# S5 parameter preparation inside a two-layer decoder trunk: dense products on VectorE, block copies on ScalarE, an earlier begin and a quota of elements

## The chip, the core and the metric

One core of a Trainium2 chip runs the whole kernel. The metric is device time in microseconds (us) of one execution, the median over runs. The kernel computes in float32; a weight or activation is split into two float32r parts (high and low), and a product of two such numbers is made of three matmuls.

## What is computed

The reference is a trunk of two layers on 256 tokens of width 1024. Each layer is a feed-forward (half weight), a mixer, and another feed-forward:

```
x = x + 1/2 W_down( silu(g) * u ),  [g u] = RMSNorm(x) W_gu        # 2816 features
x = x + W_out [ S5(u), latent attention ]                          # mixer of layer 0
x = x + 1/2 feed-forward;  x = x + 1/2 feed-forward
x = x + differential attention;  x = x + 1/2 feed-forward;  RMSNorm
```

S5 is a diagonal state-space model of 32 groups with 64 complex states and 16 channels each. With dt = exp(log_dt), a = exp(lambda dt) and f = (a - 1) / lambda its input matrix is f B, its states follow x[t] = a x[t-1] + f B u[t], and its output is Re(C x[t]) + D u[t]. All of a, f and the matrices below depend on parameters alone, not on the tokens. The kernel works on blocks of four steps, so it needs, for each of 16 pairs of groups:

- E: a^(3-i) f B for i = 0..3, which carries four inputs into the state at the end of a block (e_re, e_im, transposed);
- W: C a^d for d = 1..4, which carries a block's first state to its four outputs (w_re, w_im);
- T: Re(C a^(i-i') f B) within a block, with D on the diagonal (tmat);
- cos and sin of n theta and |a|^4, for the scan over 64 blocks (cosn, sinn, mag4).

Making these is "the preparation". They are first read in the mixer of layer 0.

## The kernel before

A planner class `Weights` (L30) streams the weights: `load` (L45) issues a DMA of 512 KB on SP into one of five stage buffers; `pre` (L54) splits a piece of 1024 columns, the high half by a ScalarE copy (L69), the low half by a VectorE subtraction (L71), and asks for the next piece. In a few places GpSimd makes the low half of a second piece.

A feed-forward (`ffn`, L264) begins with `begin` (L220): the norm of token tile 0 (`residual`, `normed`), the last products of the phase before, the transposes of tile 0 into feature-major halves yh and yl (`transpose_split`, `halves`), then the same for tile 1; `finish` transposes tile 1. The first two feature tiles are done one token tile at a time (`early`, `gate`, `turn`, L294 to L323). Then come 20 feature tiles, f = 2 to 21 (L327): 48 "up" products into gu, silu on ScalarE (L340), a product on VectorE (sh), the split of it (hs), and, two feature tiles later, 12 "down" products into acc (L280). So TensorE reads what ScalarE and VectorE make of a feature tile only two tiles later; in `early`, `gate` and `turn` there is no such distance.

The preparation is a Python generator, `setup` (L1261): the rotary tables (`rope_tables`, L445), `mixer_constants` (L424), `s5_prep` (L495). It is the `background` of the first feed-forward. After each feature tile, `ffn` advances it by a number of yields: 4 each for f below 8, 2 each below 16, 5 each below 21, and all that are left (99) at f = 21 (L351 to L354). `tc.issue_after(last)` puts what the block issues on VectorE behind `last` (the low half of hs); the other engines' instructions are not held by it. The framework then orders each engine's queue by its own estimates of readiness and by the order of the program; on the chip every queue runs strictly in order.

`s5_prep` first makes a, its powers 1 to 4 and the tables by doubling, out of operations of 16 columns and then larger ones. exp is a power of e on GpSimd (`exp_start`, L388). Then f B is made in blocks: a pair's two groups lie in the two halves of the partitions and in columns 0 to 15 and 16 to 31, with zeros elsewhere, so operations work on 64 partitions (L601) or on blocks that are half zero. The E matrices are made for eight pairs at a time with 256-column operations (L651 to L656) in the room of w_re for the first eight pairs and of w_im for the last eight; `turned_inputs` (L613) transposes them on TensorE, ScalarE copies them into e_re and e_im, and products with C give the diagonals t0 for T. Afterwards GpSimd fills w_re and w_im with the W matrices, three 512-column operations for each of eight parts (`outputs_of`, L635 to L642). Last, ScalarE places the ten blocks of tmat (L677). Helpers record their operations under their own lines: tt is L118, stt L121, ts L124.

Of the kernel before, what the change touches and what calls it, by code (L numbers as in the profile page):

```python
# [29 lines left out]
class Weights:  # L30
    """A stream of weight chunks: loaded ahead, each split exactly into two float32r parts."""
# [7 lines left out]
    def plan(self, specs):  # L39
        """specs: (array [128, n], whether it goes to the wide buffers) in the order of use"""  # L40
# [13 lines left out]
    def pre(self, other=None):  # L54
        """Splits the next chunk; other: an engine that helps with its second half."""
# [32 lines left out]
def trunk(ctx: ExitStack, tc: tile.TileContext, x, pos, invf, wff, gains, w_u, w_cq, w_ckv,  # L88
          w_uq, w_ukv, w_glu, w_out0, w_in1, w_out1, s5_lam, s5_bc, s5_d, s5_bglu, qn, kvn,
          lamv, subln, out):  # L90
    nc = tc.nc
# [24 lines left out]

    def tt(out, a, b, op):
        return nc.vector.tensor_tensor(out=out, in0=a, in1=b, op=op)  # L118

    def stt(out, a, s, b, op0, op1):  # L120
        return nc.vector.scalar_tensor_tensor(out=out, in0=a, scalar=s, in1=b, op0=op0, op1=op1)  # L121

    def ts(out, a, s1, s2_, op0, op1):
        return nc.vector.tensor_scalar(out=out, in0=a, scalar1=s1, scalar2=s2_, op0=op0, op1=op1)  # L124
# [6 lines left out]
    def behind_both(last):  # L131
        """Work that is issued after two instructions on their engines."""
# [35 lines left out]
    def rsqrt(out, a):  # L168
        """out = a ** -0.5, one column or more."""
# [14 lines left out]
    def transpose_split(src, nk, hi, lo, t):  # L184
        """token-major src [128, nk*128] -> feature-major halves, columns of token tile t."""
# [9 lines left out]
    # Phases hand the residual stream over one token tile at a time: a phase's last products for tile 0  # L195
    # come first, and those for tile 1 run while tile 0 is normalised for the next phase.
# [23 lines left out]
    def begin(prev, row):  # L220
        """prev: (last products of tile 0, those of tile 1 in pieces, the accumulators, a factor, next chunks,
# [21 lines left out]
        if acc is None:  # L243
            with tc.issue_after(last):
                ups.append(W.pre(nc.gpsimd))
# [1121 lines left out]
```

## Time and profile before

Three runs took 1045.62 to 1045.81 us, median 1045.69. The profile is of one execution; the page gives its span, 1044.7 us, and no time of its own, so about 1.0 us lie around the span.

| | share of the span |
|---|---|
| TensorE (PE) busy | 1012.1 us, 97% |
| VectorE (DVE) busy | 635.2 us, 61% |
| ScalarE (ACT) busy | 494.1 us, 47% |
| GpSimd (POOL) busy | 101.4 us, 10% |
| chain that ended last | PE 85%, DVE 6%, issue 3%, ACT 3%, POOL 1%, DMA 1% |

A busy share is a mean over stages. The first feed-forward runs from the start to about 220 us; the mixer of layer 0 follows. Where TensorE is busy without a gap at the full clock, the work of the other engines costs nothing; where it has a gap or a lower clock, the entry "idle before <- releaser" of the timeline names whom it waited for. In a timeline each entry is a run of like instructions; matmuls overlap, so the distance between two starts is the price, not the duration.

### The profile page before, as it was taken

How to read it: one execution, taken by the hardware profiler on the slowest of the kernel's cores; microseconds unless marked ns; L12 is line 12 of the kernel's file. 1: busy time of each engine (PE TensorE's matmuls, PEld its weight loads, DVE VectorE, ACT ScalarE, POOL GpSimd, SP SyncE). 2: the span in 40 equal slices, each digit the busy share in tenths (PEclk: the TensorE clock that was granted, in tenths of full speed). 3: DMA queues.
4: the chain of work that ended last, by engine and by line, in shares of the span. 5: the costliest groups of instructions: out<-in, count | busy, mean ns of one | idle time of the engine just before them, and what ended most of it. 6: DMA issues, size and time to landing. Idle time of an engine off the chain costs nothing.

```text
span 1044.7 us, 16739 instructions
## 1 busy us (share of the span) xinstructions
PE 1012.1 (97%) x6730; PEld 928.3 (89%) x6730; DVE 635.2 (61%) x1117; ACT 494.1 (47%) x848; POOL 101.4 (10%) x115
## 2 busy tenths in 40 slices
PE   7999998999979999999999999999999999999997
PEld 6999997989878899999989999999888879999996
DVE  5788778365877865555447455543757776555432
ACT  5454542455636664444336444442567756444431
POOL 3210006601510100000010000000101110000000
PEclk9999997899969999999999999999999999999999
DMA  8866663135113585555627565563453448556521
GB/s 270 262 186 196 189 190 101 51 117 187 61 41 111 192 302 182 182 184 186 209 68 263 168 217 185 189 190 140 143 180 122 143 133 290 184 184 192 187 80 40
DMA packets 49807, 174.93 MB, mean 167 GB/s; under 512 B 6081, under 2 KB 7105, under 8 KB 49730
## 3 DMA queue, kind: packets, MB, share of 16 engines
q1 hardware_dynamic: 48720, 170.46, 50.8%
q10 hardware_dynamic: 1010, 3.41, 0.9%
q8 instruction: 52, 0.85, 0.3%
q14 instruction: 25, 0.20, 0.1%
HBM read 172.80 MB, written 1.05 MB: 166 GB/s over the span
## 4 chain that ended last, share of the span: by engine, by line
PE 85%; DVE 6%; issue 3%; ACT 3%; POOL 1%; DMA 1%; SPq 0%; POOLq 0%; DVEq 0%; ACTq 0%
PE gu L336 43%; PE acc L280 22%; PE proj L685 6%; PE gt L300 3%; DVE wlo L71 2%; PE acc L696 2%; PE pu L685 1%; DVE tmat L118 1%; PE pt L190 1%; DMA xr<-in_x_dram 1%; PE ckv L685 1%; PE pz L976 1%; PE cq L685 1%; PE yp L944 1%; ACT y L199 1%
## 5 line engine op out<-in xcount | busy, mean ns | idle before, releaser
L71 DVE TENSOR_TENSOR wlo<-stage,whi 128x1024 fp32r<-128x1024 f32 x230 | 287.8, 1259 | 244.1 <-ACT whi L69 243.9
L69 ACT CAST whi<-stage 128x1024 fp32r<-128x1024 f32 (+1 forms) x236 | 240.4, 1030 | 292.5 <-issue 237.6
L336 PE MATMUL gu<-yh,whi 128*128 128x256 f32 x1280 | 363.1, 284 | 0.0
L336 PE MATMUL gu<-yh,wlo 128*128 128x256 f32 x1280 | 363.0, 284 | 0.0
L336 PE MATMUL gu<-yl,whi 128*128 128x256 f32 x1280 | 362.8, 283 | 0.0
L336 PEld LDWEIGHTS gu<-yh,whi 128*128 128x128 f32 x1280 | 246.2, 192 | 2.7
L336 PEld LDWEIGHTS gu<-yl,whi 128*128 128x128 f32 x1280 | 246.2, 192 | 2.7
L336 PEld LDWEIGHTS gu<-yh,wlo 128*128 128x128 f32 x1280 | 246.1, 192 | 0.0
L280 PE MATMUL acc<-dhi,hs 128*128 128x512 f32 x704 | 193.7, 394 | 0.0
L280 PEld LDWEIGHTS acc<-dhi,hs 128*128 128x128 f32 x704 | 128.1, 190 | 23.3 <-ACT hs L127 0.3
L71 DVE TENSOR_TENSOR dlo<-stage,dhi 128x1024 fp32r<-128x1024 f32 x88 | 108.3, 1232 | 36.3 <-ACT dhi L69 35.8
L69 ACT CAST dhi<-stage 128x1024 fp32r<-128x1024 f32 x88 | 92.3, 1050 | 68.8 <-DMA stage<-in_wff_dram 68.6
L280 PE MATMUL acc<-dlo,hs 128*128 128x512 f32 x352 | 110.9, 391 | 0.0
L280 PEld LDWEIGHTS acc<-dlo,hs 128*128 128x128 f32 x352 | 66.4, 189 | 14.4
L170 POOL TENSOR_TENSOR rs<-rs,mhalf 128x1 f32<-128x1 f32 x14 | 7.8, 557 | 658.4 <-DVE rs L124 658.4
L118 DVE TENSOR_TENSOR sh<-sh,gu 128x256 f32<-128x256 f32 x80 | 33.1, 414 | 31.8 <-ACT sh L340 31.8
L118 DVE TENSOR_TENSOR hs<-sh,hs 128x256 fp32r<-128x256 f32 x80 | 35.6, 445 | 18.7 <-ACT hs L127 18.6
L340 ACT ACTIVATE sh<-gu 128x256 f32<-128x256 f32 x80 | 30.3, 379 | 31.3 <-PE gu L336 31.3
L127 ACT CAST hs<-sh 128x256 fp32r<-128x256 f32 x80 | 32.3, 403 | 16.9 <-DVE sh L118 16.9
L685 PE MATMUL proj<-whi,yh 128*128 128x512 f32 x96 | 38.7, 403 | 0.2 <-ACT yh L127 0.2
L685 PE MATMUL proj<-wlo,yh 128*128 128x512 f32 x96 | 37.5, 391 | 0.0
L300 PE MATMUL gt<-whi,yh 128*128 128x256 f32 x128 | 34.7, 300 | 2.7 <-ACT yh L127 2.6
(326 smaller groups left out, 1138.7 us busy)
## 6 DMA issues: line engine op xcount, KB each, us to landing
stage<-in_wff_dram SPq DMA_DIRECT2D x264, 512.0 KB, 4.6
stage<-in_w_in_dram SPq DMA_DIRECT2D x24, 512.0 KB, 4.4
stage<-in_w_out_dram SPq DMA_DIRECT2D x16, 512.0 KB, 3.7
gain<-in_gains_dram ACTq DMA_DIRECT2D x6, 512.0 KB, 4.9
stage<-in_w_u_dram SPq DMA_DIRECT2D x4, 512.0 KB, 4.7
xr<-in_x_dram SPq DMA_DIRECT2D x2, 512.0 KB, 5.2
stage<-in_w_cq_dram SPq DMA_DIRECT2D x2, 512.0 KB, 4.1
stage<-in_w_ckv_dram SPq DMA_DIRECT2D x2, 512.0 KB, 4.7
```

Source lines behind the costliest of these rows:

```text
L69: nc.scalar.copy(out=hi[:, c:c + w], in_=t[:, :w])
L71: eng.tensor_tensor(out=lo[:, c:c + w], in0=t[:, :w], in1=hi[:, c:c + w].bitcast(F32), op=ALU.subtract)
L118: return nc.vector.tensor_tensor(out=out, in0=a, in1=b, op=op)
L127: copy = nc.scalar.copy(out=hi, in_=src)
L190: nc.tensor.transpose(pt[:, k, :], src[:, (k0 + k) * 128:(k0 + k + 1) * 128], ident)
L199: return nc.scalar.activation(out=y[:, sl], in_=xr[t][:, sl], func=AF.Square, scale=1.0 / 32.0, accum_out=ms[:, c:c + 1]).ins
L280: nc.tensor.matmul(acc[t][c], a[:, sl], w[:, c * 512:(c + 1) * 512], start=(f == 0 and n == 0), stop=(f == NF - 1 and n == 2))
L300: last = nc.tensor.matmul(o, a[:, k, sl], w[:, k * 256:(k + 1) * 256], start=(k0 == 0 and n == 0), stop=(k0 > 0 and n == 11))
L336: nc.tensor.matmul(gu[:, s * 256:(s + 1) * 256], w[:, k, s, :], a[:, k, :], start=(k == 0 and n == 0), stop=(k == KT - 1 and n == 2))
L340: nc.scalar.activation(out=sh[:, 0, :], in_=gu[:, :256], func=AF.Silu)
L685: last = nc.tensor.matmul(acc, a[:, k0 + k, sl], w[:, k * width:(k + 1) * width], start=(k0 == 0 and n == 0), stop=(k0 + per == nk and n = ...
L696: mm = nc.tensor.matmul(acc[t][c], a[:, k0 + k, sl], w[:, o:o + 512], start=(first and k == 0 and n == 0), stop=(last and k == 1 and n == 2))
```

## The change

- VectorE alone makes the products of the preparation, dense: all 16 pairs and all 128 partitions at once, without the zeros (`cmul_halves` on 256 columns for f B, `powers` on 768 columns for the three E powers and 1024 for the four W powers).
- `apart` on ScalarE copies the dense result into the two blocks, two copies of 64 partitions each, with the sign where one is needed. GpSimd keeps the memsets and the powers of e.
- w_re and w_im hold all E matrices, then all W matrices. `turned_inputs` works on four pairs at a time.
- The generator is given out by `aside` (until a sum of elements per partition plus 140 per tt, stt or ts reaches a quota): 3000 behind the first norm of tile 0 in the first `begin`, 2500 behind the transposes of tile 1 in `finish`, 2400 after each feature tile, and the rest at f = 21. `pause` makes a feature tile give out one step and no more.
- lam, pos and the inverse frequencies are loaded on ScalarE's DMA queue before anything else. mag4 and the second columns of cosn and sinn are copied by ScalarE.

```
+    spent = [0]
+
+    def spend(out):
+        spent[0] += math.prod(out.shape[1:]) + 140
+
     def tt(out, a, b, op):
+        spend(out)
         return nc.vector.tensor_tensor(out=out, in0=a, in1=b, op=op)
...
+    def aside(background, quota, last):
+        if background is None:
+            return
+        with tc.issue_after(last):
+            spent[0] = 0
+            while spent[0] < quota:
+                if next(background, background) is background:
+                    break
...
         if acc is None:
             with tc.issue_after(last):
                 ups.append(W.pre(nc.gpsimd))
+        aside(background, 3000, last)
         for f in second:
             f()
...
                 for _ in range(more - 1):
                     ups.append(W.pre())
+            aside(background, 2500, last[1])
             return last
...
-            if background is not None:
-                with tc.issue_after(last):
-                    for _ in range(4 if f < 8 else 2 if f < 16 else 5 if f < NF - 1 else 99):
-                        next(background, None)
+            aside(background, 2400 if f < NF - 1 else 1 << 30, last)
...
+    def first_loads():
+        nc.scalar.dma_start(out=lam, in_=s5_lam)
+        nc.scalar.dma_start(out=posi, in_=pos)
+        nc.scalar.dma_start(out=inv, in_=invf.partition_broadcast(128))
...
+        for z in (w_re, w_im):
+            nc.gpsimd.memset(z, 0.0)
...
+        for i in range(3):
+            nc.scalar.copy(out=down[:, :, i, :], in_=pw[:, :, 2 - i, :])
...
-        nc.vector.tensor_copy(out=mag4, in_=m4.unsqueeze(2).to_broadcast([128, NPAIR, NBLK]))
-        nc.vector.memset(mag4[:, :, 0:1], 0.0)
+        nc.scalar.copy(out=mag4, in_=m4.unsqueeze(2).to_broadcast([128, NPAIR, NBLK]))
+        nc.gpsimd.memset(mag4[:, :, 0:1], 0.0)
...
+        yield from cmul_halves(b_re, b_im, bc[:, 0], bc[:, 1], frb, fib, u1, u2)
+
+        def apart(dst, src, scale=1.0):
+            for j in range(2):
+                r = slice(64 * j, 64 * j + 64)
+                nc.scalar.activation(out=dst[r, :, :, 16 * j:16 * j + 16], in_=src[r], func=AF.Copy, scale=scale)
...
+        def powers(out, x, y, sx, sy, table, m, u, op):
+            sh = [128, NPAIR, m, 16]
+            for o, v, s_ in ((out, x, sx), (u, y, sy)):
+                tt(o, v.unsqueeze(2).to_broadcast(sh),
+                   table[:, s_, :m].rearrange("p d q -> p q d").unsqueeze(3).to_broadcast(sh), MUL)
+                yield
+            tt(out, out, u, op)
...
+        for dst, own, x, y, sx, sy, op in ((p_re, b_re, b_re, b_im, 0, 1, SUB), (p_im, b_im, b_re, b_im, 1, 0, ADD)):
+            yield from powers(e3, x, y, sx, sy, down, 3, u3, op)
+            apart(dst[:, :, :3], e3)
+            apart(dst[:, :, 3:], own.unsqueeze(2))
             yield
...
+        def turned_inputs(q0):
+            for src, dst in ((w_re, e_re), (w_im, e_im)):
+                tp = bank("pt").rearrange("p (k c) -> p k c", c=128)
+                for k in range(4):
+                    nc.tensor.transpose(tp[:, k, :], src[:, q0 + k], ident)
+                nc.scalar.copy(out=dst[:, q0:q0 + 4, :], in_=tp)
...
+        def pause():
+            spent[0] += 1 << 20
             yield
+        yield from pause()
+        for q0 in range(0, NPAIR, 4):
+            turned_inputs(q0)
+            yield from pause()
...
-            nc.gpsimd.tensor_tensor(out=w, in0=c_re, in1=a, op=MUL)
-            nc.gpsimd.tensor_tensor(out=g, in0=c_im, in1=b, op=MUL)
-            nc.gpsimd.tensor_tensor(out=w, in0=w, in1=g, op=ADD)
...
+        for dst, sx, sy, op, scale in ((p_re, 0, 1, SUB, 1.0), (p_im, 1, 0, ADD, -1.0)):
+            yield from powers(wd, bc[:, 2], bc[:, 3], sx, sy, pw, 4, u4, op)
+            apart(dst, wd, scale)
             yield
...
+    first_loads()
     state = (lambda: None, [], None, 1.0, [], 1)
     state = ffn(state, gains[0], setup())
```

## Rows read from the trace of the kernel before

**Rows 1.** page, slices of 26.1 us: granted TensorE clock in tenths.
```profile
PEclk9999997899969999999999999999999999999999
```

**Rows 2.** windows: us, busy (count) of PE, PEld, DVE, ACT, POOL; clock, DMA share, GB/s.
```profile
9.20:26.00 16.80, 14.93 (x106) 14.62 (x105) 12.10 (x14) 11.00 (x17) 5.25 (x3) 1.00 0.82 264
26.00:156.00 130.00, 130.00 (x926) 122.61 (x924) 105.35 (x292) 61.60 (x91) 12.81 (x12) 1.00 0.67 204
156.00:205.00 49.00, 44.10 (x272) 41.31 (x272) 30.36 (x30) 12.60 (x20) 34.91 (x25) 0.79 0.29 86
```

**Rows 3.** the same windows view, 5 us within the first dip.
```profile
175.00:180.00 5.00, 2.76 (x13) 2.07 (x11) 2.97 (x4) 0.59 (x1) 1.93 (x2) 0.50 0.42 133
```

**Rows 4.** timeline of TensorE: start us, us, instruction, [idle before <- releaser].
```profile
153.97 1.03 PE L618 MATMUL pt<-ident,w_re 128*128 128x128 f32 x8
...
159.16 0.36 PE L336 MATMUL gu<-yh,whi 128*128 128x256 f32 x1
...
167.29 0.61 PE L280 MATMUL acc<-dlo,hs 128*128 128x512 f32 x2
170.57 1.08 PE L618 MATMUL pt<-ident,w_im 128*128 128x128 f32 x4 [2.66 <-DVE w_im L118]
...
178.15 1.08 PE L618 MATMUL pt<-ident,w_im 128*128 128x128 f32 x4 [2.24 <-DVE w_im L118]
...
194.96 0.28 PE L336 MATMUL gu<-yh,whi 128*128 128x256 f32 x1
```

**Rows 5.** chain that ended last in order of time, 140 to 235 us: start, us, what.
```profile
142.88 2.75 PE acc L280 x12
...
195.12 5.75 PE gu L336 x48
```

**Rows 6.** timeline of VectorE, two operations of 256 columns.
```profile
141.82 0.43 DVE L118 TENSOR_TENSOR w_re<-tmat 128x256 f32<-128x256 f32 x1
...
163.25 1.16 DVE L118 TENSOR_TENSOR w_im<-tmat 128x256 f32<-128x256 f32 x1
```

**Rows 7.** timeline of GpSimd, the first of its products.
```profile
159.47 4.66 POOL L640 TENSOR_TENSOR w_re<-cb,s5sc 128x512 f32<-128x512 f32 x4 [80.77 <-PE t L624]
```

**Rows 8.** groups by shape, VectorE, 78 to 156 us: busy, mean ns, idle before.
```profile
L71 DVE TENSOR_TENSOR wlo<-stage,whi 128x1024 fp32r<-128x1024 f32 x20 | 24.4, 1222 | 11.8 <-ACT whi L69 11.8
```

**Rows 9.** groups by shape, ScalarE, 0 to 220 us.
```profile
L69 ACT CAST whi<-stage 128x1024 fp32r<-128x1024 f32 x46 | 47.7, 1046 | 53.2 <-issue 42.8 <-PE gu L336 7.7 <-DMA stage<-in_wff_dram 1.5
```

**Rows 10.** chain that ended last in order of time, 0 to 45 us.
```profile
2.66 6.81 DMA xr<-in_x_dram
...
11.35 5.31 PE gt L300 x24
...
26.42 5.76 PE gu L336 x48
```

**Rows 11.** windows around the two small loads of before.
```profile
12.00:14.00 2.00, 2.00 (x11) 2.00 (x11) 1.77 (x4) 1.68 (x2) 0.46 (x2) 1.00 0.56 123
14.00:16.00 2.00, 2.00 (x11) 2.00 (x10) 2.00 (x2) 0.00 (x0) 2.00 (x1) 1.00 1.01 406
```

**Rows 12.** timeline of VectorE: two independent operations, then two dependent ones.
```profile
50.69 0.17 DVE L461 COPY cc<-co 128x8 f32<-128x8 f32 x1
50.76 0.17 DVE L462 COPY cc<-co 128x8 f32<-128x8 f32 x1
...
51.65 0.17 DVE L121 SCALAR_TENSOR_TENSOR s5r<-s5kh,s5r 128x16 f32<-128x16 f32 x1
51.85 0.17 DVE L121 SCALAR_TENSOR_TENSOR s5r<-s5k,s5r 128x16 f32<-128x16 f32 x1
```

**Rows 13.** powers on GpSimd (timeline); what VectorE waited for, 26 to 60 us.
```profile
37.25 2.95 POOL L389 TENSOR_TENSOR s5w<-euler,lam 128x16 f32<-128x16 f32 x1 [21.12 <-DMA lam<-in_s_lam_dram]
40.69 4.00 POOL L389 TENSOR_TENSOR s5w<-euler,s5t 128x16 f32<-128x16 f32 x1 [0.50 <-DVE s5sc L118]
...
DVE s5sc L118 <- POOL s5w L389: 1.5, 1, 1.5
```

More of the change, by code (lines that the diff above doesn't have):

```diff
@@ L264, in ffn @@
     def ffn(prev, row, background=None):
-        yh, yl, ups, finish = begin(prev, row)
+        yh, yl, ups, finish = begin(prev, row, background)
         acc = [[None, None], [None, None]]
@@ L443, in mixer_constants @@
         ts(nlam, nlam, LAM_INIT, 1.0, SUB, MUL)
+    posi = cst.tile([128, 2], I32, name="posi")
+    inv = cst.tile([128, 24], F32, name="inv")
+    lam = cst.tile([128, 3, NPAIR], F32, name="lam")
+    def first_loads():
+        nc.scalar.dma_start(out=lam, in_=s5_lam)
+        nc.scalar.dma_start(out=posi, in_=pos)
+        nc.scalar.dma_start(out=inv, in_=invf.partition_broadcast(128))
     def rope_tables():
-        posi = cst.tile([128, 2], I32, name="posi")
-        nc.sync.dma_start(out=posi, in_=pos)
-        inv = cst.tile([128, 24], F32, name="inv")
-        nc.sync.dma_start(out=inv, in_=invf.partition_broadcast(128))
         posf = small("posf", 2)
@@ L495, in s5_prep @@
     def s5_prep():
-        lam = cst.tile([128, 3, NPAIR], F32, name="lam")
-        nc.sync.dma_start(out=lam, in_=s5_lam)
         bc = s4("bc", [128, 4, NPAIR, 16])
@@ L533, in s5_prep @@
         yield
[L535 to L536 removed]
+        ar, ai = ({d: pw[:, s, d - 1, :] for d in range(1, 5)} for s in range(2))
         t1, t2 = tmp("t1", n), tmp("t2", n)
@@ L555, in s5_prep @@
         cmul(er, ei, dr, di, dr, di, t1, t2)
-        nc.vector.memset(cosn[:, :, 0:1], 1.0)
-        nc.vector.memset(sinn[:, :, 0:1], 0.0)
-        nc.vector.tensor_copy(out=cosn[:, :, 1:2], in_=er.unsqueeze(2))
-        nc.vector.tensor_copy(out=sinn[:, :, 1:2], in_=ei.unsqueeze(2))
+        nc.gpsimd.memset(cosn[:, :, 0:1], 1.0)
+        nc.gpsimd.memset(sinn[:, :, 0:1], 0.0)
+        nc.scalar.copy(out=cosn[:, :, 1:2], in_=er.unsqueeze(2))
+        nc.scalar.copy(out=sinn[:, :, 1:2], in_=ei.unsqueeze(2))
         yield
@@ L644, in s5_prep @@
-        behind = iter(())
-        for q0 in range(0, NPAIR, 8):
-            q = slice(q0, q0 + 8)
-            held = (w_re, w_im)[q0 // 8].rearrange("p q c -> p (q c)")
-            p_re, p_im = (held[:, o:o + 1024].rearrange("p (q i c) -> p q i c", q=8, i=4) for o in (0, 1024))
-            nc.scalar.copy(out=p_re[:, :, 3, :], in_=b_re[:, q])
-            nc.scalar.copy(out=p_im[:, :, 3, :], in_=b_im[:, q])
-            for i in range(3):
-                for _ in cmul_halves(p_re[:, :, i, :], p_im[:, :, i, :], b_re[:, q], b_im[:, q],
-                                     ar[3 - i][:, q].unsqueeze(2).to_broadcast(sh),
-                                     ai[3 - i][:, q].unsqueeze(2).to_broadcast(sh), u1, u2):
-                    next(behind, None)
-                    yield
-            for _ in behind:
-                yield
-            behind = turned_inputs(q0, p_re, p_im)
@@ L660, in s5_prep @@
-        for d in range(1, 5):
-            next(behind)
-            outputs_of(w_re, d)
-            yield
-        for d in range(1, 5):
-            outputs_of(w_im, d)
+        def turned_inputs(q0):
[4 more added lines that the diff above has]
+                nc.scalar.copy(out=dst[:, q0:q0 + 4, :], in_=tp)
+            for k in range(q0, q0 + 4):
+                nc.tensor.matmul(t0[:, k, :], w_re[:, k], c_re[:, k, :], start=True, stop=False)
+                nc.tensor.matmul(t0[:, k, :], w_im[:, k], nci[:, k, :], start=False, stop=True)
```

69 lines of the change are left out of this document (21 added, 48 removed).

## The prediction

> **What bounds the kernel now.** I read the slices of the page first, then the windows, then TensorE's timeline where they differ, then the chain, and last the engines that the wait names. The clock line of the page has two dips [rows 1]; the change touches only the first, which lies at the end of the first feed-forward (20 feature tiles, f = 2 to 21, with the S5 preparation as its background). From 26 to 156 us TensorE is busy all the time at the full clock, although VectorE, ScalarE and GpSimd work on the preparation meanwhile; from 156 to 205 us it lacks 4.9 us of work and has a mean granted clock of 0.79 [rows 2]. So the preparation costs nothing until its last fifth, and then it costs twice: TensorE stands still, and afterwards it is granted half the clock (1.2 instead of 2.4 GHz) for about 20 us; one stretch of that is shown [rows 3].
>
> The timeline says what the stop is. TensorE waits 2.66 us and 2.24 us in front of its transposes for w_im, which VectorE makes [rows 4] (until the W matrices are filled, w_re and w_im each hold half of the E matrices). The price, from the same rows: between the end of one group of down products (167.29 + 0.61 = 167.90) and the feature tile that begins at 194.96 pass 27.06 us. TensorE does three things in them: the second half of the preparation's transposes and products, whose first half took 159.16 - 153.97 = 5.19 us at the full clock; one set of 12 down products, 2.75 us; one set of 48 up products, 5.75 us [rows 4, 5]. At the full clock that is 13.69 us. **The loss is 27.06 - 13.69 = 13.4 us**: 4.9 us of waits and 8.5 us of half clock.
>
> Why VectorE was late: an operation of 256 columns took 0.43 us at 142 us, and 1.16 us at 163 us [rows 6]. In the second case GpSimd was running its 512-column operations of `outputs_of`, one of which holds that engine for over a microsecond [rows 7]. The last feature tile gives out all that is left ("99"), GpSimd has nothing queued ahead of it and starts at 159.5 us, four feature tiles before that code's place. VectorE has to serve the split of the weights in the same queue, so they slip as well.
>
> **The change, part by part.** The predicted time is the median of 1045.69 less what goes, plus what comes. The profiled execution has a span of 1044.7; about 1.0 us lie around it, which I carry over.
>
> *The tail.* No elementwise product of the preparation is left on GpSimd, only memsets and powers, so the 1.16 us operations should be 0.43 again. I counted the quota through the generator (elements per partition plus 140 for each tt, stt and ts). The first `aside` gives out 41 VectorE instructions, the second 20; f = 2 to 9 carry 2580 to 3312 units each, f = 10 and 11 the three E powers each (2724), f = 12 the first pause, f = 13 to 16 one block of transposes each, f = 17 and 18 the W powers (3492 each), f = 19 the last 1304 and ten copies. Nothing is left for f = 20 and 21: there is no dump at the end. TensorE still does the same 32 transposes and 64 small products (2 x 5.19 us), but their inputs were written a feature tile earlier, so no wait stands in front of them. VectorE per feature tile: three weight splits at 1.22 and two operations of 256 columns at 0.43 are 4.5 us; the largest background, three operations of 1024 columns, is 3.7 us more [rows 6, 8]. 8.2 us fit under the 8.5 us (5.75 + 2.75) that TensorE needs per tile, narrowly. ScalarE gets `apart`, eight copies of at most 1024 columns for the W matrices at no more than 1.05 us each [rows 9], two tiles apart; the down products wait two tiles, which hides a late one. If that cover went, one stop as in rows 4 would be back (rival 3). This part: **-13.4 us**.
>
> *The loads.* lam, posi and inv leave SP, where they were issued among the weight pieces, for ScalarE's queue, ahead of the gain row. Three issues before the gain delay the broadcast of the gain, and with it the second half of y0; the first feature tile does not start with that, though: the chain of the first 45 us runs from the second half of x, landed at 9.47, over its squares to the first products at 11.35 [rows 10]. So only what delays that transfer counts. By bytes, 37 KB at 406 GB/s are 0.1 us. By the row in which small loads run, 12 to 14 us, the engines are 0.56 busy at 123 GB/s where 406 GB/s take 1.01 [rows 11]: 0.25 too much over 2 us, 0.5 us for two of the three, 0.7 us for all. I take the upper end, 0.7, since the x transfer is in flight in the same microseconds. Here the Trainium skill (DMA: Bandwidth & Descriptors, section Queues, rings and completion order) says that each DMA engine takes packets in turn from the rings of SP and ScalarE, so a load on ScalarE's ring does not line up behind SP's; by that the term is the 0.7, and by strict order of issue it would be the 0.1. The other constants are now issued behind the first five weight pieces on SP, a megabyte that SP used to issue later; what is queued behind them are pieces that wait for a free stage buffer anyway. Nothing is charged for them.
>
> *The early start.* This part costs. 61 small VectorE instructions move into the stretch from 9.2 to 26 us, where TensorE has no two tiles of slack: yl, y1, the low half of the second weight chunk and the first gate are each needed within about a microsecond. VectorE is idle there for 16.80 - 12.10 = 4.7 us [rows 2]. Independent small operations follow each other at 0.07 us, dependent ones at 0.20 us [rows 12]; some 32 of the 61 are in the two sine chains and other dependent lines. All at 0.07 are 4.3 us, under the idle time: 0. All at 0.20 with nothing between are 12.2, that is 7.5 us over it. As counted, 32 x 0.20 + 29 x 0.07 = 8.4, 3.7 over; of that I take half, 1.8 us, because the main line's operations can be issued between the links of a chain. So **+0.7 + 1.8 = +2.5 us**, with ends at 0.1 and 8.2.
>
> *The rest.* mag4, cosn, sinn and the C copies go to ScalarE or GpSimd. ScalarE is busy for 61.6 of 130 us in that stretch [rows 2], and the copies are read tiles later: nothing. The doubled `down` copy of the powers likewise.
>
> Forecast: 1045.69 - 13.4 + 2.5 = **1034.8 us**.
>
> **The rivals.**
> 1. *The start is free* (0.1): 1045.69 - 13.4 + 0.1 = 1032.4. For it: VectorE's 4.7 idle microseconds. Against: they are spread over 17 us, and a dependent line of small operations does not wait for a gap.
> 2. *VectorE waits for GpSimd's powers at the start*: 2.95 and 4.00 us on GpSimd for 16 columns; even in the slack stretch VectorE stood 1.5 us behind one [rows 13]. In the change both come before 26 us, and in VectorE's queue the gate and the third chunk's low half stand behind the waiting product, and TensorE behind these. All of it exposed is 7.0 us in place of 1.8: 1045.69 - 13.4 + 0.7 + 7.0 = 1040.0.
> 3. *The stall only moves*: 8.2 of 8.5 us at f = 17 and 18 leaves no room for a copy that VectorE must wait for (the second W power overwrites what `apart` still reads), and a weight split comes late. One stop of 2.66 us: 1037.5; with the half clock after it (8.5) 1046.0. The Trainium skill (TensorE: Matmul & The Clock Gate, Part 1) has the clock fall to half after idle time; the trace agrees, a wait of 2.66 us was followed by the 0.50 of rows 3. Against it: from 26 to 156 us VectorE was busy for 105.35 of 130 us [rows 2], 6.9 us per tile on average, and TensorE did not wait.
> 4. *Slower*: the waits of rival 2 fall into the first feature tiles, and TensorE, stopped for that long, runs at half clock for as long as in the tail. The first 24 products took 5.31 us, 0.22 each, where 48 later took 5.75 [rows 5, 10]: in the start TensorE is not at speed yet. Price 0.7 + 7.0 + 8.5 = 16.2, time 1045.69 - 13.4 + 16.2 = 1048.5. It decides the sign once the start loses over 13.4 us.
>
> **How the numbers follow.** Forecast (1033.5 to 1037) 0.56; rival 1 0.08; rival 2 0.16; rival 3 0.05 without and 0.05 with the clock; rival 4 0.10. The range takes rivals 1 and 2 and the bounds of the start: 1031.5 (rival 1 with half a microsecond for reading the loss from modelled ends) to 1041; it leaves out rival 4 and half of rival 3, 0.15. What a measurement can tell here is about 0.2%, 2 us. Faster: 0.56 + 0.08 + 0.16 + 0.05 = 0.85; the same, rival 3 with its clock, 0.05; slower 0.10.
>
> **What would show it.** Right: TensorE busy throughout 30 to 215 us at clock 1.00; no wait of its transposes for w_im; GpSimd without 512-column products; VectorE's 256-column operations at 0.43 throughout; the chain's first products 0.7 us later than 11.35, and the first up products (26.4) 2.5 us later. Wrong: a granted clock under 1 between 26 and 215 us (rival 3); VectorE idle behind GpSimd's power before 26 us with TensorE waiting (2, 4); first up products at 26.5 (1).

## The result, and the profile after

The change makes the kernel slower: median 1055.61 us of 20 runs (1048.88 to 1062.83) against 1047.34 of 20 runs of the kernel before (1045.33 to 1056.97). The ratio is 1.0063 with a 95% interval of 1.0038 to 1.0088. The prediction, 1034.8 in a range of 1031.5 to 1041.0, was wrong in sign and range. The profiled execution of after took 1059.78 us with a span of 1057.3, 12.6 more than before's 1044.7.

Three marks split these 12.6 us: the start of the first up products (gu), the first rs of the mixer's norm on VectorE, and the end.

| | before | after | difference |
|---|---|---|---|
| start to first up products | 26.3 | 40.7 | +14.4 |
| from there to the mixer's first rs | 198.7 (to 225.0) | 187.3 (to 228.0) | -11.4 |
| from there to the end of the span | 819.7 | 829.3 | +9.6 |

So the part that the prediction was built on came, and a larger loss stands in front of it. The last row is not the change's. From the mixer's first rs on TensorE runs the same 5295 matmuls in the same order in both profiles, and both fall to half clock in the mixer, in a wait of 5.41 us for xs_re; only the length differs. Windows view of the kernel before, then of after (us, then busy and count of PE, PEld, DVE, ACT, POOL, then granted clock, DMA share, GB/s):

```profile
289.00:304.00 15.00, 11.08 (x50) 10.97 (x51) 10.24 (x12) 2.52 (x6) 3.68 (x3) 0.51 0.20 70
304.00:320.00 16.00, 15.06 (x110) 13.45 (x108) 12.46 (x43) 9.75 (x28) 0.00 (x0) 0.92 0.17 56
```

```profile
295.00:329.00 34.00, 32.49 (x144) 31.16 (x145) 18.22 (x48) 10.98 (x29) 1.87 (x2) 0.50 0.18 62
```

A stretch of 17 us at half clock in the one (289.4 to 306.4), of 34 in the other. The runs of nearly every kernel here fall into one or the other kind, some 10 us apart (9 of 20 of the kernel before lie above 1050 us, 10 of 20 of after above 1057), so medians are read below beside the lowest run and the marks. Lowest run against lowest run, after is 3.55 us slower; the marks up to the mixer say 14.4 - 11.4 = 3.0.

**The end of the first feed-forward** is what the prediction said. The windows of [rows 2], now of after:

```profile
9.20:26.00 16.80, 10.55 (x37) 7.24 (x37) 10.31 (x49) 6.37 (x12) 9.89 (x8) 0.88 0.64 217
26.00:156.00 130.00, 127.83 (x906) 120.77 (x906) 94.20 (x216) 67.22 (x100) 5.51 (x4) 0.98 0.61 187
156.00:205.00 49.00, 48.66 (x356) 46.03 (x356) 27.08 (x31) 22.39 (x32) 0.00 (x0) 1.00 0.48 148
```

From 156 to 205 us TensorE is busy for 48.66 instead of 44.10 us, at clock 1.00 instead of 0.79, and GpSimd for 0.00 instead of 34.91. The transposes for w_im [rows 4] and VectorE's operations [rows 6] in the timelines of after (start us, us, instruction, [idle before <- releaser]):

```profile
165.74 0.60 PE L662 MATMUL pt<-ident,w_re 128*128 128x128 f32 x4
166.18 0.60 PE L662 MATMUL pt<-ident,w_im 128*128 128x128 f32 x4
```

```profile
189.13 0.42 DVE L124 TENSOR_TENSOR hs<-sh,hs 128x256 fp32r<-128x256 f32 x1
189.47 2.35 DVE L124 TENSOR_TENSOR tmat<-bc,pw 128x1024 f32<-128x1024 f32 x2
```

No wait stands in front of the transposes, and 256 columns take 0.42 us next to the W products.

**The start** is where the first of the windows above shows the loss: 10.55 us busy instead of 14.93 [rows 2]. TensorE's waits of over 1.4 us in the timeline of after:

```profile
8.98 3.75 PE L251 MATMUL g<-g,ones 1*128 1x512 f32 x4 [8.98 <-DMA g<-in_gains_dram]
21.40 0.38 PE L320 MATMUL gt<-whi,yh 128*128 128x256 f32 x1 [2.04 <-ACT whi L69]
26.04 1.97 PE L198 MATMUL pt<-ident,y 128*128 128x128 f32 x8 [4.25 <-DVE y L128]
37.53 0.44 PE L332 MATMUL hT<-ident,he 128*128 128x128 f32 x2 [1.48 <-DVE he L124]
```

It stands first for the gain row, and then for y of token tile 1. Behind these waits its clock is halved as well, for some 10 us (windows of after; e4, which lacks the first aside, has 1.00 from 9 to 60 us):

```profile
22.00:32.00 10.00, 5.31 (x23) 4.91 (x24) 7.98 (x20) 3.22 (x5) 3.77 (x4) 0.50 0.37 130
```

At the full clock the 5.31 us of work would be half, so the clock is at most 2.7 of the 14.4 us (an estimate from this row); the rest is waiting. What was ahead of that y in VectorE's queue (timeline of after):

```profile
22.08 0.23 DVE L450 TENSOR_SCALAR subln<-subln 128x128 f32<-128x128 f32 x1 [1.42 <-DMA subln<-in_subln_dram]
22.48 0.29 DVE L124 TENSOR_TENSOR lp<-lv 128x128 f32<-128x128 f32 x1 [0.17 <-DMA lv<-in_lamv_dram]
...
23.90 0.16 DVE L124 TENSOR_TENSOR le<-lw,lc 128x2 f32<-128x2 f32 x1 [0.61 <-POOL lw L406]
...
24.36 0.20 DVE L132 TENSOR_SCALAR rs<-ms 128x1 f32<-128x1 f32 x1
25.24 1.41 DVE L128 SCALAR_TENSOR_TENSOR y<-xr,rs,g 128x512 f32<-128x512 f32 x2 [0.67 <-POOL rs L178]
```

The rs of tile 1 comes at 24.36, behind the last line of `mixer_constants`. In the kernel before it waited for nothing but its squares (the sum that the norm needs, made on ScalarE):

```profile
10.86 0.21 DVE L124 TENSOR_SCALAR rs<-ms 128x1 f32<-128x1 f32 x1 [1.61 <-ACT y L199]
```

The chain that ended last, which in before ran over the second half of x [rows 10], now runs over the constants' loads:

```profile
2.14 6.71 DMA g<-in_gains_dram
...
14.77 0.24 SPq L50
...
15.06 0.43 SPq L442
...
16.95 5.50 DMA lv<-in_lamv_dram
22.48 0.30 DVE lp L124
...
40.84 4.20 PE gu L356 x35
```

SP stands at a weight piece for want of a free stage buffer until 14.77, issues the constants behind it, and lv lands at 22.45.

### The profile page after: what moved, and what is told of

Read it like the earlier page. It is cut to its first block, busy times and chain, and to the rows that moved or that the text cites. A ratio compares the mean times of both kernels' runs of the same rounds, so it can differ in the third digit from the quotient of the medians.

```text
span 1057.3 us, 16687 instructions
## 1 busy us (share of the span) xinstructions
PE 1016.7 (96%) x6730; PEld 932.8 (88%) x6730; DVE 617.3 (58%) x1076; ACT 505.8 (48%) x867; POOL 66.4 (6%) x87
## 4 chain that ended last, share of the span: by engine, by line
PE 81%; DVE 7%; ACT 4%; issue 3%; DMA 2%; POOL 2%; SPq 0%; ACTq 0%; DVEq 0%; POOLq 0%
PE gu L356 41%; PE acc L300 20%; PE proj L700 6%; PE gt L320 3%; DVE wlo L71 2%; PE acc L711 2%; DMA stage<-in_wff_dram 1%; PE pu L700 1%; DVE dlo L71 1%; PE yp L959 1%; PE yp L960 1%; DMA g<-in_gains_dram 1%; ACT whi L69 1%; PE ckv L700 1%; PE yp L958 1%
## 5 line engine op out<-in xcount | busy, mean ns | idle before, releaser
L71 DVE TENSOR_TENSOR wlo<-stage,whi 128x1024 fp32r<-128x1024 f32 x230 | 283.9, 1242 | 232.8 <-ACT whi L69 232.5
L124 DVE TENSOR_TENSOR hs<-sh,hs 128x256 fp32r<-128x256 f32 x80 | 33.5, 419 | 14.7 <-ACT hs L135 14.7
L320 PE MATMUL gt<-wlo,yh 128*128 128x256 f32 x128 | 35.7, 306 | 4.2 <-DVE wlo L71 4.2
```

The source lines that it names most:

```text
L71: eng.tensor_tensor(out=lo[:, c:c + w], in0=t[:, :w], in1=hi[:, c:c + w].bitcast(F32), op=ALU.subtract)
L320: last = nc.tensor.matmul(o, a[:, k, sl], w[:, k * 256:(k + 1) * 256], start=(k0 == 0 and n == 0), stop=(k0 > 0 and n == 11))
```

## The experiments

T1 in the expectations is the theory that the loss is the start, in the engines' queues; T2, that it is the late gain row alone; T3, that it is the mixer's half-clock stretch. The marks of all runs (us; rs is VectorE's, 0.3 ahead of the one on GpSimd that the expectations name; ratio to the kernel before with its 95% interval):

| kernel | first up products | rs of mixer | rest of span | median | lowest | ratio |
|---|---|---|---|---|---|---|
| before | 26.3 | 225.0 | 819.7 | 1047.34 | 1045.33 | |
| after | 40.7 | 228.0 | 829.3 | 1055.61 | 1048.88 | 1.0063 (1.0038 to 1.0088) |
| e1_gain_first | 39.8 | 230.5 | 819.6 | 1054.92 | 1048.18 | 1.0046 (1.0005 to 1.0087) |
| e2_begin_at_f2 | 28.5 | 217.5 | 829.4 | 1046.51 | 1037.49 | 0.9957 (0.9924 to 0.9989) |
| e3_loads_only | 30.0 | 229.7 | 829.9 | 1055.32 | 1050.24 | 1.0045 (1.0005 to 1.0085) |
| e4_no_first_aside | 27.3 | 219.3 | 820.8 | 1041.82 | 1039.77 | 0.9936 (0.9901 to 0.9971) |
| e5_rope_first | 32.7 | 219.7 | 819.5 | 1049.62 | 1041.55 | 0.9969 (0.9931 to 1.0006) |
| e6_constants_first | 39.1 | 228.4 | 821.2 | 1059.91 | 1050.68 | 1.0056 (1.0019 to 1.0093) |
| e7_refined | 27.7 | 213.0 | 819.4 | 1039.59 | 1034.10 | 0.9896 (0.9848 to 0.9944) |
| e8_filled | 27.0 | 212.3 | 820.0 | 1033.08 | 1031.91 | 0.9823 (0.9793 to 0.9854) |
| e9_wide_filled | 26.9 | 212.2 | 824.9 | 1039.36 | 1038.77 | 0.9900 (0.9866 to 0.9933) |
| e10_w_on_gpsimd | 28.2 | 218.0 | 820.0 | 1039.75 | 1037.29 | 0.9929 (0.9875 to 0.9982) |
| e11_constants_early | 35.5 | 222.8 | 830.0 | 1047.44 | 1043.98 | 0.9978 (0.9937 to 1.0019) |
| e12_before_filled | 25.9 | 224.6 | 820.1 | 1050.00 | 1045.92 | 1.0029 (0.9990 to 1.0067) |
| e13_after_filled | 41.3 | 231.4 | 820.1 | 1057.50 | 1051.61 | 1.0075 (1.0035 to 1.0116) |

The column "rest of span" holds 819.4 to 821.2 or 829.3 to 830.0 whatever the kernel (e9 apart), so the two marks ahead of it are the measure of each edit.

**The gain row, alone.** e1 moves one call in after; e3 moves the same three loads in before.

```
             nc.scalar.dma_start(out=g1, in_=row.unsqueeze(0))
+            first_loads()
...
-    first_loads()
     state = (lambda: None, [], None, 1.0, [], 1)
```

> The kernel after the change with one thing moved: the three small loads (lam, posi, inv) are issued on ACT's queue right behind the gain row instead of ahead of it. All asides stay. Numbers are the start of the first up products (gu, 26.4 us in the kernel before, 40.8 after), the start of the mixer's first rs (225.3 before, 228.3 after) and the whole time. T1 (the start is lost in two places, the late gain row and the first aside's instructions that stand in the engines' queues ahead of tile 1's norm): the first products come back to about 11.4, the first up products only to 34 to 37, because Sin still stands ahead of the squares of tile 1 on ACT and the work on the constants' DMAs and on GpSimd's power still stands ahead of rs of tile 1 on VectorE; mixer entry 222 to 225. T2 (the late gain row alone): up products at 26 to 29, mixer entry 213 to 217, total 1032 to 1040. T3 (the loss is not at the start but in the length of the half-clock stretch of the mixer): up products may move, but the total stays by the length of that stretch, above 1050 where it is over 25 us long, under 1045 where it is some 15 us.

```
+    def first_loads():
+        nc.scalar.dma_start(out=lam, in_=s5_lam)
+        nc.scalar.dma_start(out=posi, in_=pos)
+        nc.scalar.dma_start(out=inv, in_=invf.partition_broadcast(128))
...
+    first_loads()
     state = (lambda: None, [], None, 1.0, [], 1)
```

> The kernel before with one thing of the change: lam, posi and inv are issued on ACT's queue ahead of everything, the gain row behind them. T1: the gain row lands some 6 us later and the first products start at about 14.5 in place of 11.35, the first up products at 29 to 31 (by 3 to 4 us), and the total is 3 to 4 us above the kernel before with an equal half-clock stretch. T2: the first up products at 36 or later, the total 10 us or more above. My prediction's step (0.7 us and no more): up products at 27.1, total plus 0.7.

In e3 the first products start at 14.7 and the first up products at 30.0, 3.7 us later than in before, as T1 had it; my step had 0.7. The mixer's rs is 4.7 later, more than T1's 3 to 4. The timeline of e3:

```profile
9.21 3.75 PE L233 MATMUL g<-g,ones 1*128 1x512 f32 x4 [9.21 <-DMA g<-in_gains_dram]
```

In e1 the gain is back in time and the first products come at 9.6, but the first up products only go from 40.7 to 39.8: T2 falls, and in after the late gain is hidden behind the other loss. T1's 34 to 37 was too low, and so were its 222 to 225 for the mixer, which comes at 230.5 (e1 has one more stop, of 1.50 us at 157.74, of the kind that e13 shows below). The timeline of e1, VectorE and then ScalarE, shows why the start is late:

```profile
9.22 4.07 DVE L474 CAST posf<-posi 128x2 f32<-128x2 int32 x1
...
20.37 0.23 DVE L451 TENSOR_SCALAR subln<-subln 128x128 f32<-128x128 f32 x1 [1.59 <-DMA subln<-in_subln_dram]
21.57 0.29 DVE L124 TENSOR_TENSOR lp<-lv 128x128 f32<-128x128 f32 x1 [0.97 <-DMA lv<-in_lamv_dram]
...
23.45 0.20 DVE L132 TENSOR_SCALAR rs<-ms 128x1 f32<-128x1 f32 x1
```

```profile
16.89 0.24 ACT L398 ACTIVATE si<-rtr 128x48 f32<-128x48 f32 x1 [5.44 <-DVE rtr L132]
...
17.17 0.61 ACT L207 ACTIVATE y<-xr 128x512 f32<-128x512 f32 x1
```

The squares of tile 1 (9.49 in before) stand behind the rotary sine, and rs stands behind the constants as well.

**The asides of the first norm.** e4 is e1 without the first; e2 is e1 without both and with a quota of 3200 in place of 2400.

```
-        aside(background, 3000, last)
         for f in second:
             f()
```

> The kernel after with the small loads behind the gain row and without the first aside (the one behind the first norm's issue); the second one, at the end of the norm, stays, and so do the quota and all else. T1: with nothing queued ahead of tile 1's norm the first products are at 11.4 and the first up products at 27 to 30; mixer entry 214 to 218; total 1033 to 1039 where the mixer's half-clock stretch is some 15 us. T2: the same as in the run that only moves the gain row, within 1 us at the first up products. So the difference between these two runs is the price of what the first aside queues: 6 to 9 us by T1, none by T2.

> The kernel after with the small loads behind the gain row, with both asides of the first norm taken out, and a quota of 3200 elements in place of 2400, so that the preparation begins at the first group of up products and still ends ahead of the last. T1: the start is that of the kernel before (first products 11.4, first up products 26 to 27.5), the end of FFN 0 keeps what the change brought (no transposes waiting for w_im, clock 1.00 from 52 us on), mixer entry 212 to 216, total 1032 to 1037 where the mixer's half-clock stretch is some 15 us and up to 1045 where it is some 28. T2: the same as T1, since the gain row is on time here too. T3: no better than after by more than the stretch's length tells. If the larger quota crowds VectorE in the tiles, the up products fall behind: mixer entry 218 or later.

Without the first aside the up products start at 27.3 instead of 39.8: **the first aside costs 12.5 us**, more than the 6 to 9 expected. Both kernels end ahead of before. Both miss the mixer mark that T1 gave by 1.6 to 1.8 us (and its totals by 0.8 and 0.5 in their lowest runs), each for a reason of its own. In e4 the preparation ends one feature tile later (f = 20), and the ten copies into tmat, which the quota does not count, stand in ScalarE's queue ahead of the silu; VectorE waits 6.57 us for that, and TensorE 1.9 for hs (timeline of e4):

```profile
210.45 0.61 ACT L692 COPY tmat<-dd 32x512 f32<-32x512 f32 x1
211.09 0.38 ACT L360 ACTIVATE sh<-gu 128x256 f32<-128x256 f32 x1
```

In after the same copies stand ahead of sh of f = 20 and TensorE waits 0.9 there. In e2 the wait is 2.0 us at the first transposes of w_im, which follow its copies without a free turn (a feature tile that gives out nothing). And in both, VectorE's order has rs of tile 1 ahead of y of tile 0, so the first products come at 13.8 although the gain is there (timeline of e2):

```profile
11.04 0.21 DVE L132 TENSOR_SCALAR rs<-ms 128x1 f32<-128x1 f32 x1 [4.94 <-ACT y L207]
11.17 1.40 DVE L128 SCALAR_TENSOR_TENSOR y<-xr,rs,g 128x512 f32<-128x512 f32 x2
```

**What in the first aside costs.** e5 cuts its quota to 1 (the rotary tables), e6 puts the constants first with a quota of 600 and the tables behind them, e11 keeps all and loads bg, subln and lv on ScalarE's queue behind inv. All have the gain row first.

```
-        aside(background, 3000, last)
+        aside(background, 1, last)
```

> The kernel with the gain row first and all else as after, but the first aside stops behind the rope tables: the constants' loads are still issued there, the work on them comes in the second aside, behind tile 1's norm. Marks as before: start of the first up products (39.8 us with the full first aside, 27.3 without any). T1a (the loss is the work on late-loaded constants, which stands ahead of rs of tile 1 on VectorE: 1.6 and 1.0 us of waits for subln and lv, which land at 20.4 and 21.6, 0.6 for GpSimd's power, rs only at 23.45): rs of tile 1 comes at 12 to 15 and the up products at 27 to 30. T1b (the loss is the rope tables: the cast behind the late posi row, and Sin ahead of the squares of tile 1, 5.4 us of wait on ACT): rs of tile 1 at 18 to 19, up products at 34 to 36.

```
-        rope_tables()
         yield from mixer_constants()
+        yield
+        rope_tables()
```

> The counterpart: the first aside holds the work on the constants (subln, lv, the power of le, nlam) and nothing of the rope tables, which come in the second aside. T1a: no gain, rs of tile 1 at 23 to 24 behind the constants, as their loads are issued on SP behind the held weight piece, up products at 39 to 41. T1b: the up products come back to 28 to 32.

```
         nc.scalar.dma_start(out=inv, in_=invf.partition_broadcast(128))
+        nc.scalar.dma_start(out=bg, in_=s5_bglu)
+        nc.scalar.dma_start(out=sg, in_=subln.partition_broadcast(128))
+        nc.scalar.dma_start(out=lv, in_=lamv.partition_broadcast(128))
```

> The kernel with the gain row first and the full first aside, but bg, subln and lv are loaded on ACT's queue behind inv, in place of SP's behind the held weight piece. With these loads on SP the up products began at 39.8, and VectorE waited 1.6 us for subln and 1.0 for lv there, and 8.4 us for bg where only the constants' work stood in the first aside. If the lateness of the loads is the price: rs of tile 1 at 15 to 17.5, behind the sine chain, and the up products at 31 to 34. If it is the number of instructions queued ahead of rs, whenever their data lands: up products at 38 or later.

e6, with the constants alone, loses nearly all (39.1), as T1a had it. Its timelines, VectorE and TensorE:

```profile
20.30 0.17 DVE L450 TENSOR_SCALAR bg<-bg 128x4 f32<-128x4 f32 x1 [8.37 <-DMA bg<-in_s_bglu_dram]
22.29 0.23 DVE L451 TENSOR_SCALAR subln<-subln 128x128 f32<-128x128 f32 x1 [1.83 <-DMA subln<-in_subln_dram]
```

```profile
26.23 1.97 PE L198 MATMUL pt<-ident,y 128*128 128x128 f32 x8 [10.44 <-DVE y L128]
```

The waits for two small loads, bg and subln, hold VectorE for 10.2 us, and TensorE waits 10.44 us for the y behind them. e5, with the tables alone, starts its up products at 32.7, between the two theories: taking the constants out gives back 7.1 us, the tables keep 5.4 of the 12.5. In e5 GpSimd is in the way. Timelines of e5, VectorE and then GpSimd:

```profile
10.75 3.12 DVE L478 TENSOR_SCALAR ang<-inv,posf 128x24 f32<-128x24 f32 x2
17.34 0.75 DVE L128 SCALAR_TENSOR_TENSOR y<-xr,rs,g 128x512 f32<-128x512 f32 x1 [2.10 <-POOL rs L178]
```

```profile
12.01 1.81 POOL L524 MEMSET w_im<- 128x2048 f32 x1
13.77 2.92 POOL L407 TENSOR_TENSOR s5w<-euler,lam 128x16 f32<-128x16 f32 x1
```

The two operations for ang, 0.36 us in after, take 3.12, although inv had landed at 10.6; they end at 13.87, 0.05 us behind GpSimd's memset of w_im. In e1 the cast above, 0.18 us in after, takes 4.07 and ends at 13.29, 0.03 us behind the same memset. Then rs of tile 1 stands on GpSimd behind the power of e, which ends at 16.69, and y waits 2.1 us for it. No run moves this GpSimd work alone, so its share of the 5.4 us is read from the rows and not tested.

So neither T1a nor T1b holds alone. The two losses lie over each other: the constants by themselves would be 11.8 (39.1 - 27.3), the tables 5.4, both together 12.5. e11 confirms the lateness of the loads for a part only: 35.5, where the lateness alone would have given 31 to 34 and the mere number of instructions 38. At least 4.3 of the 12.5 go with the loads' place (the edit has a price of its own, since ScalarE issues three more loads ahead of its first squares and rs of tile 0 comes at 7.64 instead of 5.81), and the work on them still stands in the queue: rs of tile 1 comes at 18.71, behind the chain of the rotary sine.

**The refined kernel.** e7 loads lam, posi and inv on SP in the preparation as before did, has no aside in the norm, a quota of 3800, one more empty turn before the transposes, tmat's copies over three turns, and rs of tile 1 behind y of tile 0:

```
-        y1, last = normed(1, *r1, g)
+        with tc.issue_after(first_y) if acc is None else ExitStack():
+            y1, last = normed(1, *r1, g)
...
         yield from pause()
+        yield from pause()
         for q0 in range(0, NPAIR, 4):
...
+            if i0 < 2:
+                yield from pause()
```

> What the runs so far suggest: lam, posi and inv are loaded on SP in the preparation, as in the kernel before; no aside in the first norm; the quota is 3800 elements from the first up products on; one more empty turn ahead of the transposes and the ten copies into tmat given out over three turns; rs of tile 1 is tied behind y of tile 0, which stood ahead of it in the kernel that begins at f = 2 (first products 13.8 there). T1: first products at 11.4, first up products at 26.3 to 27, no PE wait of over 1 us from there to the mixer, mixer entry 212.5 to 215, and from there 819 us with the short half-clock stretch or 829 with the long one: a span of 1032 to 1034 or of 1042 to 1044. If the larger quota crowds VectorE ahead of f = 10, PE waits for hs or sh there and the entry is at 217 or later.

Mixer mark, waits and span are as T1 expected; the first products came at 11.9 (11.4 expected) and the first up products at 27.7, 0.7 us past the range. From the first up products to the mixer's rs it takes 185.3 us, 13.4 less than before. Windows of e7:

```profile
52.00:212.00 160.00, 160.00 (x1138) 150.28 (x1137) 108.47 (x223) 85.96 (x133) 2.89 (x3) 1.00 0.54 168
```

**GpSimd beside VectorE.** e10 is e7 with the products of the W matrices on GpSimd.

```
-        def powers(out, x, y, sx, sy, table, m, u, op):
+        def powers(out, x, y, sx, sy, table, m, u, op, eng=nc.vector):
...
-            tt(out, out, u, op)
+            spend(out)
+            eng.tensor_tensor(out=out, in0=out, in1=u, op=op)
...
-            yield from powers(wd, bc[:, 2], bc[:, 3], sx, sy, pw, 4, u4, op)
+            yield from powers(wd, bc[:, 2], bc[:, 3], sx, sy, pw, 4, u4, op, nc.gpsimd)
```

> The refined kernel with the six products of each W matrix on GpSimd in place of VectorE, at the same turns (f = 16 and 17); nothing else. The theory behind the term of 13.4 us (VectorE beside a GpSimd that streams wide operands runs at some 0.4 of its speed): while GpSimd holds these products, VectorE's operations of 256 columns take 0.8 us or more in place of 0.42 and its splits of 1024 columns over 2 us in place of 1.22, and TensorE waits in these tiles; FFN 0 ends 2 us or more later. The rival, that before's loss came only from the order of the work (the transposes behind too much VectorE work): operations of 0.42 and 1.22 as in the refined kernel, and no later end.

The contention that the 13.4 us rested on is there. GpSimd, with an empty queue, starts the W products at 113 us, far ahead of their turn, as outputs_of did in before [rows 7]. Timelines of e10, GpSimd, VectorE, TensorE:

```profile
118.28 3.27 POOL L645 TENSOR_TENSOR tmat<-tmat 128x1024 f32<-128x1024 f32 x1
```

```profile
119.21 2.62 DVE L124 TENSOR_TENSOR hs<-sh,hs 128x256 fp32r<-128x256 f32 x1
121.76 3.04 DVE L71 TENSOR_TENSOR dlo<-stage,dhi 128x1024 fp32r<-128x1024 f32 x1
```

```profile
126.32 0.58 PE L356 MATMUL gu<-yh,whi 128*128 128x256 f32 x1 [1.70 <-DVE sh L124]
```

An operation of 0.42 us takes 2.62, a split of 1.22 takes 3.04; TensorE waits, its clock falls to 0.77 in the 10 us from 120 to 130, and the mixer begins 5.0 us later (0.5 of it ahead of the first up products). That is its price here; what it was of the 13.4 in before, beside the order of the work, this run does not tell. The Trainium skill (SBUF — State Buffer, section SBUF: two separate sides) says that a VectorE operation with two SBUF inputs and a GpSimd operation that reads SBUF exclude each other for a whole instruction instead of sharing a rate. The rows agree: the 0.42 us operation that started at 119.21 ended at 121.83, just behind GpSimd's, which ended at 121.55.

**The mixer's half clock.** e8 is e7 with twenty repeats of the first narrow product in the wait for xs_re; e9 has six of 512 columns there instead; e12 and e13 put the twenty into before and after.

```
             for q in range(8):
                 k = 8 * b + q
+                for _ in range(20 if k == 0 else 0):
+                    nc.tensor.matmul(yp[:, q, :], tmat[:, k, :], u[:, k, :], start=True, stop=True)
```

> The same with twenty more products of the first S5 block (tmat by u into the region that the real first product then overwrites), queued on PE in the place where it waits 5.4 us for xs_re. T3 (the half-clock stretch of the mixer follows from this wait, and its length, 17 or 30 to 37 us in the profiles, is what splits the runs in two groups 10 us apart): clock 1.00 from 276 to 340 or a stretch under 8 us, one group of times instead of two, and 5 to 9 us below the faster group of the run without the filling. If the clock falls for what happens ahead of that wait, the stretch stays, the split stays, and the times are those of the run without the filling.

> The refined kernel with another filling of the mixer's wait: in place of twenty products of 64 columns (with which the clock still fell, some 6 us later, for 17 us) six products of 512 columns, into the same region that the real products overwrite. If narrow products leave TensorE too little to do to be granted the full clock, the clock stays 1.00 through the filling and the half-clock stretch is shorter than 17 us or gone, and the time is 2 to 8 us under that with the narrow filling (1033.1). If the stretch follows from the 24 narrow products behind the wait, whatever fills it, it begins later, lasts as long, and the time is within 2 us of 1033.

> The kernel before with the twenty narrow products in the mixer's wait and nothing else. With them in the refined kernel all runs lay within 2.3 us, where without them they fell in two groups 10 us apart. If the filling takes the long half-clock stretch away whatever the kernel: one group of times, at 1043 to 1047, no run at 1051 or above. If the one group was an accident of the refined kernel's timing: two groups again, some 10 us apart.

> The kernel after with the same filling and nothing else. If the filling levels the stretch, the change is seen without it: one group at 1046 to 1050, 3 us above the kernel before with the filling (the difference of the two kernels at the mixer's entry, 228.3 against 225.3), in place of the 8 us between the medians without the filling. If the change itself lengthens the stretch: 8 to 12 us above, or two groups with most runs in the higher.

T3 in its simple form falls. With the narrow filling the clock still falls, some 4 us later, for 17 us, and the lowest run is 2.2 us under that of e7 and not 5 to 9; windows of e8:

```profile
281.00:298.00 17.00, 16.91 (x75) 15.97 (x74) 9.30 (x27) 6.73 (x18) 0.18 (x1) 0.51 0.18 63
```

With the wide one it stays at 1.00 through the first S5 block, whose products take half the time. It falls at 291.3, some 11 us later than in e8, at the end of a wait of 2.37 us in the attention with another of 2.43 behind it; windows of e9:

```profile
279.00:291.00 12.00, 9.65 (x74) 8.40 (x72) 11.93 (x24) 4.74 (x10) 2.01 (x2) 1.00 0.40 119
291.00:311.00 20.00, 17.26 (x77) 16.29 (x78) 7.56 (x28) 6.50 (x21) 0.00 (x0) 0.51 0.09 35
```

That is no gain: 824.9 us behind the mark instead of the 820.0 of e8, and 1039.4 instead of 1033.1. All six runs of e8 lay at 1031.9 to 1034.1, but e12 and e13 fall into two groups again (1045.9 to 1046.9 and 1053.1 to 1055.9; 1051.6 to 1053.3 and 1057.5 to 1062.4). So the filling does not take the long stretch away, and e8's even times are no proof of it. What decides the length stays open. The Trainium skill (TensorE: Matmul & The Clock Gate, Part 1) has the clock gate watch the engine at a rhythm of its own that a kernel's start does not reset; lengths that differ between runs of one program fit that, and no run here shows it.

e13 also shows one way in which after's runs come to lie over 3 us above before's where the stretch is equal: its mixer mark is 6.8 us past that of e12, not 3.0. It has one more stop, 1.45 us of TensorE behind sh at 158.83 with a clock of 0.85 behind it to 170 us, which e1 has and after's profiled run does not (0.34 us). The chain of e13 there:

```profile
151.44 3.54 DMA stage<-in_wff_dram
...
155.00 1.05 ACT dhi L69
```

A weight piece lands late, and VectorE's split of it stands ahead of sh. So the change's own loss is 3 to 7 us in a run.

## Why the prediction failed

- *The tail, -13.4: right in mechanism and in size, 2 us short in this kernel.* The stretch got 11.4 us shorter in after and 13.4 in e7. The step that missed is "the down products wait two tiles, which hides a late one": I charged nothing for the last turn's ten copies, and they delay a silu, not a copy. TensorE shows 0.85 us for it in after and 1.88 in e4; another 0.34 are the wait at 157 us, and 0.8 stand in no wait over 0.3 us and stay open. e10 shows the contention that the term rested on.
- *The loads, +0.7: mis-sized, 3.7 to 4.7 alone (e3).* The failed sentence is "only what delays that transfer counts". I took the gain row for late by three issues, 1.4 us; TensorE read it 6.05 us later (issued at 2.14, 6.71 us on its way and read at 8.98; in before issued at 0.74 and read at 2.93), and with that the broadcast, both halves of y and the transposes are late, which the chain of before [rows 10] had hidden by little. The rule of the Trainium skill that I weighed (DMA: Bandwidth & Descriptors, section Queues, rings and completion order) is about turns between queues, and the row now stood behind three loads on its own; no run here shows how the two queues shared the engines. Nor was the 0.7 read from the right row: the two small loads of before, issued at 12.6 and 13.1, landed 4.4 and 4.1 us later, outside the 12 to 14 us of [rows 11].
- *"Nothing is charged for them", the constants behind the weight pieces: the step that decided the sign.* I looked at what stands behind these loads on SP, not at who reads them. `mixer_constants` reads them in the first aside, so VectorE, in order, waits until 22 us for them with rs of tile 1 behind it (e6: 10.2 us of waits). With the gain in time, moving these loads alone takes the mixer's rs from 230.5 (e1) to 222.8 (e11), from behind the 225.0 of before to ahead of it; 4.3 of that lie ahead of the first up products, and without e1's extra stop (3.4 by the same marks) e1 would still be behind.
- *The early start, +1.8 with ends at 0 and 7.5: 12.5 (e4 against e1).* I counted 61 instructions by their durations against VectorE's idle 4.7 us. Their durations are a part of it (e11: rs of tile 1 at 18.71 though the loads are early), but the waits came on top: for the loads, and on ScalarE a sine that waits 5.44 us for VectorE ahead of the squares, while VectorE stands beside GpSimd (4.07 us for a cast in e1). Behind them came the half clock. The bounds of this term held no wait for a load, none for GpSimd and no clock.
- *The rivals.* Rival 4 had the right turning point, a start that loses over 13.4 us, and a clock that falls with it (0.50 from 22 to 32 us), at 0.10. That its 1048.5 lies beside the lowest run of after, 1048.88, is luck, since its mechanism was not the one: in after GpSimd's powers held VectorE for 0.6 and 2.7 us, and the one wait of TensorE behind them is 1.48 us, where the late gain held VectorE for 5.0 us (0.7 in before) and, in e6, the loads of the constants for 10.2.
- *What would show it.* Of the signs listed as right, transposes, GpSimd and the 256-column operations came, and the clock from 41 us on (1.00 to 215 us, with TensorE busy for 173.66 of 174); from 30 to 41 it was 0.90, a sign listed as wrong. The first products came at 14.46 instead of 12.05 and the first up products 14.4 us later instead of 2.5.

## What to carry to other kernels

An instruction moved early costs what it waits for, and not only what it lasts: for each one look up who writes its inputs, when that lands, and which critical instruction then stands behind it in the same in-order queue. Of a load, follow its reader, not its neighbours. Background work is best begun where its inputs have landed anyway and TensorE has tiles of slack; e8 and e7, which do that, are the fastest here, 1.8% and 1.0% under the kernel before; a part of e8's is that none of its six runs had the long half-clock stretch, for which no reason is shown.

## What was not expected of the hardware

- A row of 4 KB on ScalarE's DMA queue took 6.71 us from issue to landing behind 37 KB of small loads on that queue (after); in front of them TensorE had read it 2.2 us after its issue (e2).
- Next to one GpSimd operation of 3.27 us, VectorE's operation of 256 columns grew from 0.42 to 2.62 us (e10): it waits the other one out. A cast of 2 columns took 4.07 us instead of 0.18 beside GpSimd's low half of a weight piece and the memset behind it, and ended 0.03 us after that (e1).
- The half-clock stretch of the mixer comes in lengths of 14 to 17 us (e13, before) and 34 to 37 us (after, e3), worth 10 us of 1047; before and after differ so for the same order of TensorE's matmuls. It began in the wait for xs_re where that was empty, some 4 us later where twenty narrow products stood in it, and at the end of the next wait (2.37 us) where six wide ones did, there for 20 us.
